# Attention: block maxima taken two at a time, row sums formed one unit later, heads divided in pairs

## The chip, the cores and the metric

The kernel runs on one core of one Trainium2 chip. The metric is the device time of one execution in microseconds (us); the median of the runs shown is 2695.03 us.

## The reference

One layer of a bidirectional encoder with 2048 tokens of width 1024, all in float32: a mixer sub-layer (8 query heads over 2 key heads of width 64, beside a pooling mixer, and one output projection) and a gated feed-forward sub-layer with a convolution of width 3. The change is in the attention:

```python
q = q * (1.0 / math.sqrt(HEAD_DIM))
s = jnp.einsum('bqkgd,bskd->bkgqs', qblk, k)
p = jax.nn.softmax(s, axis=-1)
o = jnp.einsum('bkgqs,bskd->bqkgd', p, v)
...
mix = jnp.concatenate([att, pool], axis=-1) @ w_out[l]
x = x + g1 * mix
h2 = rmsnorm(x, norm2_g[l]) * (1.0 + sc2) + sh2
```

The softmax needs three things for each query: the maximum of its 2048 scores, the exponentials' sum, and the weighted sum of the values divided by it.

## The kernel before, in words

Operands are split into a high part that TensorE takes exactly and a low rest, so that products come out close to float32. A stage ahead of the attention (spans 0 to about 380 us) projects queries, keys, values and pooled channels and writes them to DRAM; a stage behind it (from about 1240 us) is the feed-forward part.

The attention goes through 32 units: 4 chunks of 512 queries (QC) times 8 heads. `gen_unit(u)` walks over 16 blocks of 128 keys (kt). For each it makes the scores S in one of three banks of PSUM (L731, L732; the second matmul adds minus the row maximum, which sits in row 64 of `qb`), two exponentials on ScalarE (ph, rounded, L735, and the full one in place, L736), their difference pl on VectorE (L737), and two steps behind it the products with the values: `pv` adds ph times values into bank A (L723) and pl times values and ones into bank B (L724). The sum of ph over the keys goes two ways: GpSimd adds up the first 13 blocks in `acc` (L739, L741), and for the last three (ONE_PE) TensorE multiplies ph with ones into B (L726). At the unit's end acc is split into ah (ScalarE, L751) and al (VectorE, L752), and two more matmuls with ones add these to B (L757, L758). Then ScalarE copies half of A and the row of sums out of the banks (L765, L766), VectorE adds the halves into `o1` (L767, L768), and the row of sums goes through DRAM by four DMAs on SP's queue: out, back as 128x4, reciprocal on VectorE (L776), out, and back spread over 64 partitions as `rb` (L774 to L778). `finish(u)`, called in step 10 of the next unit, multiplies o1 by rb into one half of `att` (L798) and, with every second head, splits att into atth (ScalarE) and attl (GpSimd, L802).

`gen_max(u+1)` runs beside unit u, one step of it to each step of the unit: 16 matmuls pmx (4 query tiles times 4 blocks of 512 keys, L692), each into one of two banks with the tag mx, and each followed by a maximum over its 512 columns on VectorE (L694). Then the 16 partial maxima of the four query tiles become nm (L697), four small matmuls turn it into a row in a bank with the same tag (L701), and ScalarE copies that row into qb (L702). Without it the next unit's L732 cannot run.

Beside the units run the fillers of `plan`: matmuls of the output projection (`gen_half`, L820) into the one bank misc, whose result VectorE adds to x (L842), and `ln2_early`, the norm ahead of the feed-forward part: sum of squares on ScalarE (L849), root on GpSimd (L120, L121), scaling of a 128x1024 tile on VectorE (L853), and eight transposes on TensorE (tp, L860).

The Python generators give a written order. The framework's scheduler takes it as the priority and issues, on each engine, the first instruction that it takes to be ready at that time, so each engine's final order is fixed in the program and can differ from the written one. It also places every wait. A tile of a tag with `bufs=1` can be written again only when all that read the last one are done.

## Time and profile before

| | before |
|---|---|
| median of 3 runs | 2695.03 us (2693.51 to 2695.31) |
| the profiled execution | 2694.41 us |
| its span, first to last instruction | 2692.6 us |
| TensorE matmuls busy | 2577.8 us (96%) |
| VectorE, ScalarE, GpSimd busy | 1926.2, 1544.4, 1615.7 us |

The profiled execution lies 0.6 us below the median, and its span 1.8 us below its own time. The attention takes the stretch from 385 to 1240 us, 855 us for 32 units, which is 26.7 us for one; stretches are named by their start and end in this span. The durations of neighbouring matmuls overlap in the records: a matmul of 512 columns is shown with 0.40 us, but the next one starts 0.23 us behind it.

### The profile page before, as it was taken

Reading aid. Unit: us, or ns where it says so; the run is one execution under the profiler, and the core shown is the slowest. Engines: PE = TensorE matmul, PEld = TensorE weight load, DVE = VectorE, ACT = ScalarE, POOL = GpSimd, SP = SyncE. Lnnn points to the kernel's source line nnn. Section 1 sums busy time; section 2 is a strip of 40 time slices with the busy share of each in tenths; the row PEclk is TensorE's granted clock in tenths of the full one; section 3 lists DMA queues with packets and bytes.
Section 4 is the critical chain, followed back from the end, with each engine's and each line's share of the span. In section 5 each row is a group of like instructions: output and inputs, shape, how many; then the busy total and the mean of one; then the engine's idle time right before and its main releaser. Section 6 shows DMA issues by size and latency. Waiting matters only on the chain.

```text
span 2692.6 us, 38997 instructions
## 1 busy us (share of the span) xinstructions
PE 2577.8 (96%) x13439; PEld 2232.5 (83%) x13439; DVE 1926.2 (72%) x3014; ACT 1544.4 (57%) x2848; POOL 1615.7 (60%) x1397
## 2 busy tenths in 40 slices
PE   5899989999999999989899999899999999999999
PEld 5788877777776776767898999699999998999998
DVE  7877678889999999888577776745555557455554
ACT  5565457767778777776654555554343445544442
POOL 1222135656566666664887887586565676777673
PEclk9999989999999999999999999999999999999999
DMA  9685373431222122223544444533332325333332
GB/s 293 233 266 180 100 242 103 149 100 58 71 63 77 58 76 69 78 88 120 172 149 135 148 132 139 195 106 103 105 106 94 95 78 189 114 122 118 110 110 86
DMA packets 318161, 338.61 MB, mean 126 GB/s; under 512 B 24656, under 2 KB 226330, under 8 KB 317962
## 3 DMA queue, kind: packets, MB, share of 16 engines
q1 hardware_dynamic: 316953, 332.31, 39.1%
q0 software_dynamic: 1008, 3.81, 0.5%
q8 instruction: 105, 1.72, 0.3%
q14 instruction: 95, 0.77, 0.1%
HBM read 249.42 MB, written 86.63 MB: 125 GB/s over the span
## 4 chain that ended last, share of the span: by engine, by line
PE 47%; DVE 2%; POOL 1%; ACT 1%; issue 1%; DMA 0%; DVEq 0%; SPq 0%; POOLq 0%; ACTq 0%
PE py L1248 16%; PE px L1159 13%; PE pw L1159 9%; PE pz L1159 8%; PE pl L1377 1%; DVE b L993 0%; POOL wl_s L1035 0%; ACT hb L977 0%; POOL t L1000 0%; DVE y L1253 0%; DMA wr<-in_w_up_dram 0%; POOL t L1007 0%; POOL wl_a L1035 0%; ACT ac L1218 0%; DVE t L993 0%
## 5 line engine op out<-in xcount | busy, mean ns | idle before, releaser
L741 POOL TENSOR_TENSOR acc<-acc,ph 128x512 f32<-128x512 f32 x352 | 463.6, 1317 | 40.7 <-ACT ph L735 15.5
L1035 POOL TENSOR_TENSOR wl_s<-s,wh_s 128x512 fp32r<-128x512 f32 x260 | 349.6, 1346 | 204.7 <-ACT wh_s L1033 202.1
L735 ACT ACTIVATE ph<-S 128x512 fp32r<-128x512 f32 x512 | 306.9, 600 | 130.0 <-PE S L732 114.3
L737 DVE TENSOR_TENSOR pl<-S,ph 128x512 fp32r<-128x512 f32 x512 | 348.0, 683 | 40.0 <-ACT S L736 33.0
L1253 DVE TENSOR_TENSOR y<-py,y 128x512 f32<-128x512 f32 x300 | 205.8, 688 | 222.4 <-PE py L1248 220.7
L694 DVE TENSOR_REDUCE mx<-pmx 128x1 f32<-128x512 f32 x500 | 337.4, 680 | 25.9 <-PE pmx L692 23.9
L1033 ACT CAST wh_s<-s 128x512 fp32r<-128x512 f32 x264 | 163.5, 621 | 313.0 <-PE pw L1159 146.8
L1035 POOL TENSOR_TENSOR wl_a<-wr,wh_a 128x512 fp32r<-128x512 f32 x195 | 266.7, 1374 | 104.7 <-ACT wh_a L1033 104.3
L736 ACT ACTIVATE S<-S 128x512 f32<-128x512 f32 x512 | 306.5, 599 | 0.0
L1248 PE MATMUL py<-wdh,gh 128*128 128x512 f32 x664 | 261.7, 395 | 1.9 <-DVE y L1253 1.7
L1248 PE MATMUL py<-wdh,gl 128*128 128x512 f32 x664 | 262.1, 395 | 0.0
L1248 PE MATMUL py<-wdl,gh 128*128 128x512 f32 x664 | 261.8, 395 | 0.0
L1033 ACT CAST wh_a<-wr 128x512 fp32r<-128x512 f32 x198 | 122.3, 618 | 240.8 <-PE pz L1159 202.4
L1159 PE MATMUL px<-t,wh_s 128*128 128x322 f32 (+1 forms) x1024 | 247.9, 322 | 5.3 <-ACT p1s L1192 3.6
L724 PE MATMUL B<-pl,vt 128*128 128x512 f32 x512 | 210.5, 411 | 5.3 <-DVE pl L737 5.0
L723 PE MATMUL A<-ph,vt 128*128 128x512 f32 x512 | 204.6, 408 | 5.3 <-ACT ph L735 5.3
L692 PE MATMUL pmx<-kA,qa 128*128 128x512 f32 x500 | 203.2, 408 | 3.4 <-DMA kA<-k_scr 2.5
L732 PE MATMUL S<-qb,kB 65*128 65x512 f32 x512 | 202.8, 402 | 1.1 <-ACT qb L702 0.8
L731 PE MATMUL S<-qa,kA 128*128 128x512 f32 x512 | 202.4, 398 | 0.0
L739 POOL TENSOR_TENSOR acc<-ph,ph 128x512 f32<-128x512 f32 x32 | 41.3, 1290 | 255.4 <-ACT ph L735 234.9
L1159 PEld LDWEIGHTS px<-t,wh_s 128*128 128x128 f32 x1024 | 178.3, 189 | 12.3 <-ACT p1s L1192 4.4
L1159 PE MATMUL px<-t,wl_s 128*128 128x322 f32 (+1 forms) x512 | 164.2, 321 | 0.0
(297 smaller groups left out, 6877.9 us busy)
## 6 DMA issues: line engine op xcount, KB each, us to landing
wr<-in_w_up_dram SPq DMA_DIRECT2D x132, 512.0 KB
wdh<-wd_scr SPq DMA_DIRECT2D x88, 256.0 KB
wdl<-wd_scr SPq DMA_DIRECT2D x88, 256.0 KB
stage<-in_w_ada_dram SPq DMA_DIRECT2D x36, 512.0 KB
x_scr<-x SPq DMA_DIRECT2D x48, 256.0 KB
wds<-in_w_down_dram SPq DMA_DIRECT2D x44, 256.0 KB
wd_scr<-wdh SPq DMA_DIRECT2D x44, 256.0 KB
wd_scr<-wdl SPq DMA_DIRECT2D x44, 256.0 KB
```

Of the source, the lines that this page charges most:

```text
L694: V.tensor_reduce(out=mx[:, qt, j:j + 1], in_=ps, axis=AX.X, op=ALU.max)
L723: PE.matmul(A, vt[:, kt, 192 * a:192 * a + P], ph, start=kt == 0, stop=kt == NKT - 1)
L724: PE.matmul(B, vt[:, kt, 64 + 64 * a:192 + 64 * a], pl, start=kt == 0, stop=False)
L735: S.activation(out=ph, in_=s, func=AF.Exp, scale=0.125)
L736: S.activation(out=s, in_=s, func=AF.Exp, scale=0.125)
L737: V.tensor_tensor(out=pl, in0=s, in1=ph.bitcast(F32), op=ALU.subtract)
L741: G.tensor_tensor(out=acc, in0=acc, in1=ph.bitcast(F32), op=ALU.add)
L1033: S.copy(out=hf, in_=src)
L1035: eng.tensor_tensor(out=lf, in0=src, in1=hf.bitcast(F32), op=ALU.subtract)
L1159: mm = PE.matmul(ps, l_[:, k], r_[:, k, 0:N], start=first and k == 0 and m == 0, stop=k == 3 and m == 2, skip_group_check=not first)
L1248: PE.matmul(ps, l_[:, ts_], r_, start=i == 0, stop=i == 3 * len(js) - 1)
L1253: V.tensor_tensor(out=ys[t][:, ns], in0=ps, in1=ys[t][:, ns], op=ALU.add)
```

## The change

- `gen_max` takes pmx in pairs: two matmuls fill a tile of 2 x 512 columns (two banks, tag mx, now `bufs=1`), and one VectorE maximum goes over all 1024 columns. A unit has 8 such maxima instead of 16, and nm reads 8 columns instead of 16. The row of L701 takes a pair tile too.
- GpSimd adds up ph of all 16 blocks (ONE_PE applies to the last unit alone), and al is made on GpSimd instead of VectorE. The three matmuls per unit of ph with ones go.
- The two matmuls with ah and al no longer go into B at the unit's end. `sum_up(u-1)`, called in step 3 of the next unit, makes them into a pair tile of tag mx; ScalarE copies one row of it out, and DRAM now takes two rows (one from B, one from this tile), which come back as 128x2x4 and are added ahead of the reciprocal: five DMAs instead of four, and one more small VectorE instruction. ah and al keep their slots (tags ph with 4, pl with 3) until then.
- VectorE adds B straight into `att`; one multiplication 128x512 for two heads takes the place of two of 64x512, and `finish` comes in step 13 instead of 10.
- The scaling in `ln2_early` goes from VectorE to GpSimd.
- The last unit keeps the old way; two tail halves of the output projection wait for the last `sum_up`.

```diff
 
+        def mx_pair(nm):
+            return ps2.tile([P, 2, 512], F32, tag="mx", name=nm, bufs=1)
+
         def gen_max(u):
             c_, h = units[u]
             a = h // 4
             qa, qb = qtiles[u]
-            mx = p2.tile([P, 4, 4], F32, tag="mx", name=f"mx{u}", bufs=2) if u else mx0
-            for jq in range(0 if u else 4 * JP, 16):
-                for j, qt in ((jq // 4, jq % 4) if u == 0 else (jq % 4, jq // 4),):
-                    ps = ps2.tile([P, 512], F32, tag="mx", name=f"pmx{u}_{qt}_{j}", bufs=2)
-                    PE.matmul(ps, qa[:, qt * P:(qt + 1) * P], kA[:, a, j * 512:(j + 1) * 512],
+
+            def pair(nm):
+                return mx_pair(f"{nm}{u}")
+
+
+            mx = p2.tile([P, 4, 2], F32, tag="mx", name=f"mx{u}", bufs=2) if u else mx0
+            for i in range(8 if u else 2):
+                ps = pair(f"pmx{i}_")
+                for t in range(2):
+                    qt, j = (i // 2, 2 * (i % 2) + t) if u else (2 * i + t, JP)
+                    PE.matmul(ps[:, t], qa[:, qt * P:(qt + 1) * P], kA[:, a, j * 512:(j + 1) * 512],
                               start=True, stop=True)
-                    V.tensor_reduce(out=mx[:, qt, j:j + 1], in_=ps, axis=AX.X, op=ALU.max)
+                    if u == 0:
+                        V.tensor_reduce(out=mx[:, qt, j:j + 1], in_=ps[:, t], axis=AX.X, op=ALU.max)
                     yield
+                if u:
+                    V.tensor_reduce(out=mx[:, qt, i % 2:i % 2 + 1], in_=ps.rearrange("p a n -> p (a n)"),
+                                    axis=AX.X, op=ALU.max)
             nm = p2.tile([P, 4], F32R, tag="nm", name=f"nm{u}", bufs=2)
             V.tensor_reduce(out=nm, in_=mx, axis=AX.X, op=ALU.max, negate=True)
-            row = ps2.tile([P, 512], F32, tag="mx", name=f"row{u}", bufs=2)
+            row = pair("row")[:, 0]
             yield
             for qt in range(4):
                 PE.matmul(row[0:1, qt * P:(qt + 1) * P], nm[:, qt:qt + 1], identr, start=True, stop=True)
...
             first = []
+            final = u == NU - 1
 
             def pv(kt, ph, pl):
                 PE.matmul(A, vt[:, kt, 192 * a:192 * a + P], ph, start=kt == 0, stop=kt == NKT - 1)
-                PE.matmul(B, vt[:, kt, 64 + 64 * a:192 + 64 * a], pl, start=kt == 0, stop=False)
-                if kt >= NKT - ONE_PE:
+                PE.matmul(B, vt[:, kt, 64 + 64 * a:192 + 64 * a], pl, start=kt == 0,
+                          stop=kt == NKT - 1 and not final)
+                if final and kt >= NKT - ONE_PE:
                     PE.matmul(B, onesr[:, o64], ph, start=False, stop=False)
 
             for kt in range(NKT):
...
                 V.tensor_tensor(out=pl, in0=s, in1=ph.bitcast(F32), op=ALU.subtract)
                 if kt == 1:
                     G.tensor_tensor(out=acc, in0=first[0].bitcast(F32), in1=ph.bitcast(F32), op=ALU.add)
-                elif 1 < kt < NKT - ONE_PE:
+                elif 1 < kt < NKT - (ONE_PE if final else 0):
                     G.tensor_tensor(out=acc, in0=acc, in1=ph.bitcast(F32), op=ALU.add)
                 first.append(ph)
                 pend.append((kt, ph, pl))
...
             while pend:
                 if len(pend) == 1:
                     S.copy(out=ah, in_=acc)
-                    EA.tensor_tensor(out=al, in0=acc, in1=ah.bitcast(F32), op=ALU.subtract)
+                    (V if final else G).tensor_tensor(out=al, in0=acc, in1=ah.bitcast(F32), op=ALU.subtract)
                 pv(*pend.pop(0))
                 yield
-            for _ in range(XY):
-                yield
-            PE.matmul(B, onesr[:, o64], ah, start=False, stop=False)
-            PE.matmul(B, onesr[:, o64], al, start=False, stop=True)
+            if final:
+                PE.matmul(B, onesr[:, o64], ah, start=False, stop=False)
+                PE.matmul(B, onesr[:, o64], al, start=False, stop=True)
             dr = slice(64 * a, 64 * a + 64)
             rr = slice(64 - 64 * a, 128 - 64 * a)
             r0 = 64 - 64 * a
+            lo = 64 * (h % 2)
+            if h % 2 == 0:
+                att["f"] = p2.tile([P, QC], F32, tag="att", name=f"att{u}", bufs=1), \
+                    p2.tile([P, QC], F32, tag="rb", name=f"rb{u}", bufs=1)
+            at, rb = att["f"]
...
             S.copy(out=o1[dr], in_=A[rr])
             S.copy(out=o1[r0:r0 + 1], in_=B[r0:r0 + 1])
             V.tensor_tensor(out=o1[dr], in0=A[dr], in1=o1[dr], op=ALU.add)
-            V.tensor_tensor(out=o1[dr], in0=B[dr], in1=o1[dr], op=ALU.add)
...
+            V.tensor_tensor(out=at[lo:lo + 64], in0=B[dr], in1=o1[dr], op=ALU.add)
             SP.dma_start(out=r_scr[u, 0], in_=o1[r0:r0 + 1])
-            SP.dma_start(out=rc, in_=r_scr[u, 0].rearrange("o (p i) -> (o p) i", i=4))
-            V.reciprocal(out=rc, in_=rc)
-            SP.dma_start(out=r_scr[u, 1].rearrange("o (p i) -> (o p) i", i=4), in_=rc)
-            SP.dma_start(out=rb[dr], in_=r_scr[u, 1].broadcast_to([64, QC]))
-            open_units[u] = (o1, rb, dr)
-            yield
+            open_units[u] = (o1, dr, at, rb)
+            sums[u] = (ah, al, o64, r0)
+            yield
+
+        def sum_up(u):
+
+            ah, al, o64, r0 = sums.pop(u)
+            o1, dr, at, rb = open_units[u]
+            lo = 64 * (units[u][1] % 2)
+            rs = mx_pair(f"rs{u}")[:, 0]
+            PE.matmul(rs, onesr[:, o64], ah, start=True, stop=False)
+            PE.matmul(rs, onesr[:, o64], al, start=False, stop=True)
+            r1 = r0 + 32
+            S.copy(out=o1[r1:r1 + 1], in_=rs[r1:r1 + 1])
+            SP.dma_start(out=r_scr[u, 1], in_=o1[r1:r1 + 1])
+            rc = p2.tile([P, 2, 4], F32, tag="rc", name=f"rc{u}", bufs=2)
+            SP.dma_start(out=rc, in_=r_scr[u, 0:2].rearrange("n o (p i) -> (o p) n i", i=4))
+            V.tensor_tensor(out=rc[:, 0], in0=rc[:, 0], in1=rc[:, 1], op=ALU.add)
+            V.reciprocal(out=rc[:, 0], in_=rc[:, 0])
+            SP.dma_start(out=r_scr[u, 2].rearrange("o (p i) -> (o p) i", i=4), in_=rc[:, 0])
+            SP.dma_start(out=rb[lo:lo + 64], in_=r_scr[u, 2].broadcast_to([64, QC]))
+            if u == NU - 2:
+                last_sum.append(u)
 
...
-            E = V if u == NU - 1 else E1
-            E.tensor_tensor(out=at[lo:lo + 64], in0=o1[dr], in1=rb[dr], op=ALU.mult)
-            if h % 2 == 1:
-                S.copy(out=ah[:, h // 2], in_=at)
-                E = V if u == NU - 1 else E2
-                E.tensor_tensor(out=al[:, h // 2], in0=at, in1=ah[:, h // 2].bitcast(F32),
-                                op=ALU.subtract)
+            last = u == NU - 1
+            if last:
+                row = o1[64 - dr.start:65 - dr.start]
+                rl = ps2.tile([P, 512], F32, tag="A", name="rb_last", bufs=1)
+                PE.matmul(rl, ones[64 - dr.start:65 - dr.start, :], row, start=True, stop=True)
+                V.tensor_tensor(out=at[0:64], in0=at[0:64], in1=rb[0:64], op=ALU.mult)
+                V.tensor_tensor(out=at[64:128], in0=o1[dr], in1=rl[dr], op=ALU.mult)
+            else:
+                V.tensor_tensor(out=at, in0=at, in1=rb, op=ALU.mult)
+            S.copy(out=ah[:, h // 2], in_=at)
+            E = V if last else E2
+            E.tensor_tensor(out=al[:, h // 2], in0=at, in1=ah[:, h // 2].bitcast(F32), op=ALU.subtract)
...
-            V.tensor_scalar(out=x1, in0=x1, scalar1=r, scalar2=None, op0=ALU.mult)
+            eng.tensor_scalar(out=x1, in0=x1, scalar1=r, scalar2=None, op0=ALU.mult)
             for _ in range(wait[1]):
                 yield
             for q in range(2):
...
                     step(filler)
                     frac -= 1
-                if n == 10 and u > 0:
+                if n == 3 and u > 0:
+                    sum_up(u - 1)
+                if n == 13 and u > 0:
                     finish(u - 1)
                 if n == 2:
```

## Rows read from the trace of the kernel before

**Rows 1.** The page: busy time, share of the span and instructions of each engine.

```profile
PE 2577.8 (96%) x13439; PEld 2232.5 (83%) x13439; DVE 1926.2 (72%) x3014; ACT 1544.4 (57%) x2848; POOL 1615.7 (60%) x1397
```

**Rows 2.** Busy time by stretch: the attention's four quarters, and all of it.

```profile
core 0: us, PE busy (x) PEld busy (x) DVE busy (x) ACT busy (x) POOL busy (x), PEclk, DMA share, GB/s
385.00:600.00 215.00, 211.09 (x894) 163.89 (x894) 190.54 (x314) 155.50 (x287) 128.64 (x99) 0.98 0.44 140
600.00:816.00 216.00, 214.05 (x924) 165.62 (x922) 197.35 (x327) 162.05 (x302) 132.34 (x102) 1.00 0.23 69
816.00:1022.00 206.00, 198.32 (x845) 145.41 (x844) 191.62 (x316) 165.22 (x312) 135.62 (x112) 1.00 0.23 67
1022.00:1240.00 218.00, 208.18 (x888) 156.04 (x889) 189.58 (x307) 166.54 (x315) 135.76 (x114) 0.98 0.26 74
385.00:1240.00 855.00, 831.63 (x3548) 630.94 (x3548) 769.08 (x1260) 649.30 (x1216) 532.37 (x427) 0.99 0.29 88
```

**Rows 3.** Waits in 385 to 1240: us in total, times, longest.

```profile
PE tp L860 <- DVE lx L853: 6.0, 7, 2.0
PE A L723 <- ACT ph L735: 5.3, 16, 0.9
PE B L724 <- DVE pl L737: 5.0, 15, 0.6
PE po L820 <- DVE x L842: 0.4, 1, 0.4
...
DVE rc L776 <- DMA rc<-r_scr: 1.3, 2, 0.8
...
POOL acc L739 <- ACT ph L735: 234.9, 30, 10.8
```

**Rows 4.** Groups of 385 to 1240: count, busy us, mean ns, idle before, what ended it.

```profile
L741 POOL TENSOR_TENSOR acc<-acc,ph 128x512 f32<-128x512 f32 x352 | 463.6, 1317 | 40.7 <-ACT ph L735 15.5 <-PE pmx L692 0.9
...
L726 PE MATMUL B<-ph,onesr 128*128 128x512 f32 x96 | 38.0, 396 | 0.0
...
L798 DVE TENSOR_TENSOR att<-o,rb 64x512 f32<-64x512 f32 x31 | 36.8, 1186 | 0.7
...
L842 DVE TENSOR_TENSOR x<-po,x 128x512 f32<-128x512 f32 x48 | 32.6, 680 | 0.2
...
L752 DVE TENSOR_TENSOR al<-acc,ah 128x512 fp32r<-128x512 f32 x32 | 21.7, 679 | 0.0
L802 POOL TENSOR_TENSOR attl<-att,atth 128x512 fp32r<-128x512 f32 x15 | 19.3, 1288 | 0.0
...
L853 DVE TENSOR_SCALAR lx<-lx,rstd 128x1024 f32<-128x1024 f32 x12 | 11.0, 920 | 2.1 <-POOL rstd L121 2.1
```

**Rows 5.** Timeline of one unit's end: start, us, engine, line, operation, count, idle before.

```profile
628.38 0.40 PE L726 MATMUL B<-ph,onesr 128*128 128x512 f32 x1
628.61 0.40 PE L757 MATMUL B<-ah,onesr 128*128 128x512 f32 x1
628.85 0.40 PE L731 MATMUL S<-qa,kA 128*128 128x512 f32 x1
629.24 0.51 PE L758 MATMUL B<-al,onesr 128*128 128x512 f32 x1
629.58 0.40 PE L701 MATMUL row<-identr,nm 128*1 128x128 f32 x4
...
627.90 0.68 DVE L694 TENSOR_REDUCE mx<-pmx 128x1 f32<-128x512 f32 x1
628.50 0.68 DVE L752 TENSOR_TENSOR al<-acc,ah 128x512 fp32r<-128x512 f32 x1
629.10 0.16 DVE L697 TENSOR_REDUCE nm<-mx 128x4 fp32r<-128x16 f32 x1
...
629.78 0.58 ACT L766 COPY o<-B 1x512 f32<-1x512 f32 x1 [1.61 <-PE B L758]
630.38 0.57 ACT L702 CAST qb<-row 1x512 fp32r<-1x512 f32 x1
```

## What the change should do to the time

> **What bounds the kernel now.** I read the busy times first: TensorE's matmuls fill 96% of the span, no other engine more than 72% [rows 1]. Then the stretches of the attention [rows 2]: of 855 us TensorE is busy 831.6, the other 23 are lost in small pieces, and VectorE is next with 769, or 90%. VectorE's share overstates it: in the timeline its 512-column instructions are shown with 0.68 us and start 0.60 apart (627.90, 628.50, 629.10), so about a tenth of its rows is overlap [rows 5]. GpSimd is busy 62%. A matmul is shown with 0.40 us, and the next starts 0.23 behind it (628.38, 628.61, 628.85) [rows 5]; 0.23 is what one more or less costs while TensorE has work. Last come the waits: of the named ones of TensorE the largest are the transposes on the scaled tile, 6.0 us, ph, 5.3, and pl, 5.0 [rows 3]. So TensorE is the bound, and a matmul saved is time saved, except where TensorE waits anyway. That place is a unit's end [rows 5]: acc, split into ah and al, goes as matmul L758 into B, ScalarE's copy out of B (629.78) stands waiting for it 1.61 us, and the copy that gives the next unit its maxima (630.38) stands in ScalarE's queue behind that; TensorE's starts there are 0.39 and 0.34 apart instead of 0.23.
>
> **The matmuls.** Three per unit go (96 of L726 in 32 units [rows 4], 93 after the change took all but the last unit's). The ah and al matmuls stay, but move into the next unit. At 0.233: 93 x 0.233 = 21.7 us, if all of it is on the path. At the unit's end five matmuls go, 1.17 us, and two come back in the next unit's body, 0.47. What the end then waits for is VectorE: in [rows 5] the last maximum starts at 627.90, al at 628.50, nm at 629.10. Without al, nm can start 0.6 earlier, and the copy into qb no longer queues behind the copy out of B; that one took 0.58 from 629.78, so the row's copy comes about 0.9 earlier in all. If the end is bound by this chain, a unit gains 0.9 - 0.47 = 0.43 us, 13 us in 31 units; if TensorE's queue finds other work for the rest, 21.7. The written order need not be the issued one: in [rows 5] a score matmul of the next unit (628.85) already stands ahead of this unit's L758, so most holes are filled. I take 18.
>
> **The paired maxima.** The maximum over 1024 columns isn't in the trace. The same operation takes 0.68 on 512 and 0.16 on 16 columns [rows 5]; in a straight line that gives 0.68 + 512 x (0.68 - 0.16)/496 = 1.22 us, and start to start 1.14 instead of 2 x 0.60. That frees 8 x 0.06 = 0.5 us of VectorE per unit; al gives 0.60 more, and one multiplication of two heads instead of two (1.19 each [rows 4]) about 0.6; a small add of 128x4 costs under 0.16. Some 1.5 of 26.7 us. VectorE isn't the bound, so only waits for it shrink: those of L724 on pl, 5.0 us, and part of others [rows 3]. I take 3 us, between 0 and 10.
>
> **One pair tile instead of two banks.** This is the added wait. The first matmul of a pair must wait for the maximum over the pair ahead of it, and what is queued behind it on TensorE waits with it: the next scores, and so ScalarE and VectorE. From the start of a pair's second matmul the next pair can start after 0.40 (the matmul), some 0.3 (VectorE in the midst of a 0.60 instruction), 1.22 and a little: 1.96 us. In the written order there lie four matmuls of S, A and B and about 1.5 of filler between them, 5.5 x 0.233 = 1.28. The lack of 0.68 is covered if three more matmuls are issued in front. A unit has some 26 us for eight rounds of 0.23 + 1.96 = 2.2, 17.5 in all, the row and the new sums each one round more: there is room. The nearest row for one buffer handed back and forth is the misc bank: written 48 times behind VectorE's addition (L842 [rows 4]), TensorE waited 0.4 us for that in all [rows 3]. That rate on 248 pairs gives 2 us; I take 3, and keep 53 as the far end, which is 0.21 us for each of the 248, two matmuls moved in front and not three.
>
> The Trainium skill (PSUM — Partial Sum Buffer, Summary: rules for kernel authors) says to read PSUM in a different bank from the one that a running matmul targets. Both kernels keep to that, but before it was two buffers in turn and now it is two banks held as one buffer; by that rule alone this edit is a loss, and it is the first rival below.
>
> **GpSimd.** It gets three additions (1.317 each) and al (shape of attl, 1.288) per unit [rows 4]: 5.24 x 8 = 42 us per quarter, so 171 to 178 of 206 to 218 [rows 2]. The cover is its idle time ahead of each unit's first addition, 234.9 us in 30 waits, 7.8 each [rows 3]. If that cover were short, its lateness would hold ph's four slots (of which ah now keeps one for a third of a unit), and ScalarE behind them: 0 to 16 us. I take 0. Twelve scalings of 128x1024 move to it. Here they take 0.92 [rows 4]; GpSimd has none of that shape, two inputs of 512 take 1.3, so up to 2.6 for 1024, and no less than the 0.75 or so that the other engine takes undisturbed. So -2 to +20 us if every bit of it reaches the transposes, which waited for this tile 6.0 us [rows 3]; I take +3.
>
> The Trainium skill (GPSIMD Engine Reference, 4.1 Engine selection) gives elementwise work to VectorE, with GpSimd about 2 times slower on two inputs. The rows agree on al: 0.679 on VectorE, 1.288 on GpSimd. It calls one input roughly line rate, which for 1024 columns would be an estimate of 1.1 us, and my 3 would be 2.
>
> **What I cost at nothing.** The extra ScalarE copy per unit (0.58, 18 us in all) lies beside ScalarE's idle 24%. The fifth DMA and the later sums: the chain now starts some 9 us into the unit and has 10 us up to step 13 for two round trips; the reciprocal waited 1.3 us in 31 times [rows 3], and only every second unit needs the result in step 13. If the multiplication stood waiting on VectorE, pl and the maxima would queue behind it, some 2 us each time, 16 times, 32 us. SP's loads for units three ahead have room to be late. The last two tail halves and step 13 cost nothing for the same reason.
>
> **The sum.** -18 - 3 + 3 + 3 = -15 us. From the profiled execution, 2694.4, that is 2679.4; the median stands 0.6 higher, so 2680.0.
>
> **Rivals.** (1) The pair tile is the bound, slower: TensorE stands before each pair. For it: 0.68 us short in the written order, and the scheduler's order is fixed ahead, so what comes late by a tenth on the chip is waited for. Against it: the misc bank. It decides the sign from 18 us, 0.073 us a pair; at 0.21 it gives -18 - 3 + 53 + 3 = +35, 2730. (2) No change: GpSimd paces the units. Fifteen additions, al, half an attl and the wait for ah (0.6) make 19.8 + 1.3 + 0.6 + 0.6 = 22.3, in the last two quarters some 1.5 more, of 26.7; should each unit wait 0.5 us for it, 16 us go, and 2696 is left. That would also be the answer if the unit's end were limited by its chain and one other cost of the list came in full: 2680 + 5 + 11. (3) More than forecast: the chain from acc through B to the row's copy was what disturbed TensorE most, and with a lighter VectorE half of its lost 23 us comes back: -21.7 - 12 = -34, 2661. (4) Slower through the late scaling on GpSimd or the later sums, +20 or +32 less 15: 2690 to 2712.
>
> **Chances.** The forecast, about 8 to 25 us faster, 0.42; (3) 0.18; (2) 0.15; (1) 0.17; (4) 0.08, all but a little of it slower. A difference of under 0.2%, 5.4 us, can't be told from none. Faster 0.60, same 0.15, slower 0.25. The range takes in (2), (3) and (1) at its price and leaves out a worse loss or a bigger gain: 2656 to 2730. The forecast's own range is 2670 to 2687.
>
> **What would show it.** Right: 31 units shorter by 0.4 to 0.7 us; L726 left with three matmuls; a 1024-column maximum of about 1.22; waits of L692 on the maximum under 10 us; the copy into qb close behind its row; GpSimd's wait ahead of L739 down from 7.8 to some 2 to 3 us a unit. Wrong: waits of pmx on mx of tens of us, or ph waiting for acc for tens of us, the transposes for the scaled tile, or the multiplication of L798 for rb. The stages outside the attention must keep their lengths; if they don't, the forecast misses something that I haven't seen.

## The result: 3% slower, and the profile after

The changed kernel takes 2773.51 us (median of four runs, 2772.99 to 2780.99), the kernel before 2694.27 beside it: a ratio of 1.0301, 95% interval 1.0282 to 1.0319, or 79 us more. The forecast was 2680 with a range of 2656 to 2730: wrong in sign, and the time lies above the range.

| | before | after |
|---|---|---|
| span of the profiled execution | 2692.6 us | 2771.3 us |
| granted clock, mean | 0.988 | 0.975 |
| up to the attention's first score matmul | 378.3 us | 376.0 us |
| first to last score matmul of the attention | 856.8 us | 934.8 us |
| from there to the first feed-forward product | 39.4 us | 44.2 us |
| the rest | 1418.1 us | 1416.3 us |

Of the 78.7 us between the spans the 32 units have 78.0, or 2.4 us a unit. The last unit's end has 4.8 more, the other stages a little less than before. The page's first line, as in [rows 1], shows 93 matmuls fewer, as planned, VectorE relieved by 40 us, and GpSimd with 193 us more:

```profile
PE 2596.3 (94%) x13346; PEld 2226.5 (80%) x13346; DVE 1885.7 (68%) x2739; ACT 1563.2 (56%) x2879; POOL 1808.7 (65%) x1533
```

PE's busy time rose although its matmuls fell. That is mostly the clock: 326 matmuls start at its lower level in this kernel, 163 in the one before. The stretches of the attention's four chunks, as in [rows 2] (columns: stretch, its length, busy time and instructions of each engine, granted clock, DMA share, GB/s):

```profile
core 0: us, PE busy (x) PEld busy (x) DVE busy (x) ACT busy (x) POOL busy (x), PEclk, DMA share, GB/s
376.00:607.00 231.00, 214.84 (x879) 159.41 (x877) 184.74 (x250) 159.79 (x297) 167.04 (x132) 0.95 0.45 142
607.00:831.00 224.00, 212.73 (x889) 157.96 (x888) 185.92 (x253) 162.83 (x306) 175.59 (x136) 0.99 0.24 66
831.00:1069.00 238.00, 205.44 (x832) 145.62 (x830) 182.17 (x246) 172.57 (x325) 190.53 (x149) 0.95 0.21 60
1069.00:1316.00 247.00, 219.46 (x873) 160.09 (x874) 178.35 (x244) 173.40 (x325) 190.00 (x148) 0.92 0.20 60
376.00:1316.00 940.00, 852.46 (x3469) 623.09 (x3468) 731.18 (x990) 668.59 (x1248) 723.16 (x563) 0.95 0.27 82
```

GpSimd, the one that got more, is busy 723 of 940 us and so not full; TensorE is busy 852 of them, a smaller share than before. The loss grows to the end: the last two chunks are the slowest (238 and 247), and in them lie eleven of the twelve scalings. What TensorE, VectorE, ScalarE and GpSimd waited for between 385 and 1330 us (us in total, times, longest), against [rows 3]:

```profile
PE row L714 <- DVE nm L710: 27.6, 17, 4.4
PE tp L897 <- POOL lx L890: 16.9, 7, 4.8
PE S L748 <- ACT qb L715: 11.5, 13, 3.2
PE A L738 <- ACT ph L751: 6.0, 12, 1.7
PE po L857 <- DVE x L879: 5.8, 8, 1.4
PE pmx L701 <- DVE mx L707: 4.5, 9, 1.6
PE B L739 <- DVE pl L753: 3.3, 9, 0.6
DVE att L837 <- DMA rb<-r_scr: 1.4, 3, 0.9
ACT ah L767 <- POOL acc L757: 59.9, 31, 4.1
POOL acc L755 <- ACT ph L751: 114.1, 30, 13.5
POOL al L768 <- ACT ah L767: 17.5, 24, 0.7
```

The first line is new: the row of maxima waits for its VectorE result in 17 units (before: once, 1.0 us). So is the wait of ScalarE's copy ah for GpSimd's last addition, in all 31 units that add all 16 blocks on GpSimd (before: once, 0.3 us). The groups that answer to [rows 4] (count, busy us, mean ns, idle before and what ended it):

```profile
L707 DVE TENSOR_REDUCE mx<-pmx 128x1 f32<-128x1024 f32 x248 | 301.7, 1216 | 79.0 <-PE pmx L701 78.6
L890 POOL TENSOR_SCALAR lx<-lx,rstd 128x1024 f32<-128x1024 f32 x12 | 34.3, 2859 | 1.2
L768 POOL TENSOR_TENSOR al<-acc,ah 128x512 fp32r<-128x512 f32 x31 | 39.7, 1282 | 17.5 <-ACT ah L767 17.5
L701 PEld LDWEIGHTS pmx<-kA,qa 128*128 128x128 f32 x497 | 92.2, 197 | 46.6 <-DVE mx L707 15.7 <-ACT o L807 11.7 <-DVE mx L704 1.3
```

The fourth line is easily missed. In the list of waits a matmul pmx waits 4.5 us for maxima, but its weight load, which comes first on the engine, waits 15.7 for maxima and 11.7 for the copy of the late sums (L807), which sit in the same tile: a wait can stand at the load and not at the matmul. Now one unit's end in the timeline, as in [rows 5] (start, us, engine, operation, idle before):

```profile
898.90 1.29 POOL L757 TENSOR_TENSOR acc<-acc,ph 128x512 f32<-128x512 f32 x1
...
900.22 0.62 ACT L767 CAST ah<-acc 128x512 fp32r<-128x512 f32 x1 [2.14 <-POOL acc L757]
900.86 0.59 ACT L783 COPY o<-A 64x512 f32<-64x512 f32 x1
901.48 0.68 DVE L785 TENSOR_TENSOR o<-A,o 64x512 f32<-64x512 f32 x1 [1.96 <-ACT o L783]
902.09 1.21 DVE L707 TENSOR_REDUCE mx<-pmx 128x1 f32<-128x1024 f32 x1
903.33 0.68 DVE L792 TENSOR_TENSOR att<-B,o 64x512 f32<-64x512 f32 x1
904.04 0.16 DVE L710 TENSOR_REDUCE nm<-mx 128x4 fp32r<-128x8 f32 x1
904.35 0.40 PE L714 MATMUL row<-identr,nm 128*1 128x128 f32 x4 [2.57 <-DVE nm L710]
904.79 0.58 ACT L715 CAST qb<-row 1x512 fp32r<-1x512 f32 x1 [2.74 <-PE row L714]
```

Read it from the top: GpSimd ends its last addition at 900.19. ScalarE's ah stands next in ScalarE's order and has waited 2.14 us for it; the copy of A stands behind ah; VectorE's addition behind that copy; the last maximum behind that addition, though its matmuls were done long before (the pair at 899.53); then nm, the row, which TensorE waits 2.57 us for, and qb, without which no score of the next unit ends. An addition on GpSimd, which no product of this unit needs any more, has become the head of the chain into the next unit through the fixed orders of two other engines. Over the 31 units the addition ends 2.70 us behind the end of the sixteenth ph (before: 2.17 ahead of it), nm starts 4.10 behind it (before 2.56), and the next unit's first score matmul on qb 6.49 (before 4.79).

**A budget of TensorE's time.** Since waits stand in several places, I added them up at one: in the attention (from 20 us behind the first score matmul to 3 us behind the last), each start-to-start distance of neighbouring matmuls beyond 0.2335 us (0.11 for the narrow ones), booked to the matmul that starts late; what is due to a granted clock of 0.5 is booked apart. Records that are missing count as lost, so a few us are uncertain.

| us lost | all | half clock | row | pmx | tp | S | A, B | po |
|---|---|---|---|---|---|---|---|---|
| before | 48.9 | 2.0 | -3.9 | 3.7 | 10.5 | 7.8 | 22.5 | 4.8 |
| after | 143.6 | 16.9 | 25.7 | 23.0 | 20.8 | 17.8 | 25.5 | 12.6 |

After has lost 94.7 us more. Less 93 matmuls at 0.2335, 21.7, that makes 73.0 of the 78.0, so in this account the saved matmuls were paid out in full and the losses are over four times as large. They are the row (+30), pmx (+19), half clock (+15), tp (+10), S (+10) and po (+8). Three parts of the change can be behind them: three more blocks on GpSimd, the one pair tile, and the scaling on GpSimd. The experiments take them one by one.

### The profile page after: what moved, and what is told of

The parts are those of the page before. It is cut to its first block, busy times and chain, and to the rows that moved or that the text cites. A ratio compares the mean times of both kernels' runs of the same rounds, so it can differ in the third digit from the quotient of the medians.

```text
span 2771.3 us, 38990 instructions
## 1 busy us (share of the span) xinstructions
PE 2596.3 (94%) x13346; PEld 2226.5 (80%) x13346; DVE 1885.7 (68%) x2739; ACT 1563.2 (56%) x2879; POOL 1808.7 (65%) x1533
## 4 chain that ended last, share of the span: by engine, by line
PE 45%; DVE 2%; POOL 1%; ACT 1%; issue 1%; DMA 0%; DVEq 0%; POOLq 0%; ACTq 0%
PE py L1295 15%; PE px L1206 12%; PE pw L1206 8%; PE pz L1206 8%; PE pl L1424 1%; DVE b L1040 0%; POOL wl_s L1082 0%; ACT hb L1024 0%; POOL t L1047 0%; DVE y L1300 0%; POOL wl_a L1082 0%; POOL t L1054 0%; DVE ac L1268 0%; DMA h_scr<-ht 0%; DMA wr<-in_w_up_dram 0%
## 5 line engine op out<-in xcount | busy, mean ns | idle before, releaser
L757 POOL TENSOR_TENSOR acc<-acc,ph 128x512 f32<-128x512 f32 x445 | 578.4, 1300 | 69.4 <-ACT ph L751 40.9
L707 DVE TENSOR_REDUCE mx<-pmx 128x1 f32<-128x1024 f32 x248 | 301.7, 1216 | 79.0 <-PE pmx L701 78.6
L748 PE MATMUL S<-qb,kB 65*128 65x512 f32 x512 | 212.2, 415 | 12.3 <-ACT qb L715 11.5
L738 PE MATMUL A<-ph,vt 128*128 128x512 f32 x512 | 214.8, 426 | 7.5 <-ACT ph L751 6.0
L701 PE MATMUL pmx<-kA,qa 128*128 128x512 f32 x500 | 182.9, 426 | 11.6 <-DVE mx L707 4.5
L120 POOL TENSOR_SCALAR rstd<-ss 128x1 f32<-128x1 f32 (+1 forms) x48 | 20.0, 416 | 207.7 <-ACT junk L276 100.9
```

The lines of the kernel that those rows point to most:

```text
L707: V.tensor_reduce(out=mx[:, qt, i % 2:i % 2 + 1], in_=ps.rearrange("p a n -> p (a n)"), axis=AX.X, op=ALU.max)
L738: PE.matmul(A, vt[:, kt, 192 * a:192 * a + P], ph, start=kt == 0, stop=kt == NKT - 1)
L748: PE.matmul(s, kB[0:65, a, ks], qb[0:65], start=False, stop=True)
L757: G.tensor_tensor(out=acc, in0=acc, in1=ph.bitcast(F32), op=ALU.add)
```

## Experiments: one part taken back from the changed kernel

Each kernel is given with its ratio to the kernel before, timed beside it. The diffs of this section stand against the changed kernel.

**The three blocks back on TensorE in every unit** (the late sums and al stay as changed):

```diff
-                if final and kt >= NKT - ONE_PE:
-                    PE.matmul(B, onesr[:, o64], ph, start=False, stop=False)
+                if kt >= NKT - ONE_PE:
+                    PE.matmul(B, onesr[:, o64], ph, start=False, stop=kt == NKT - 1 and not final)
...
-                elif 1 < kt < NKT - (ONE_PE if final else 0):
+                elif 1 < kt < NKT - ONE_PE:
```

> The kernel after with ONE_PE = 3 in every unit: GpSimd adds up 13 blocks again and TensorE multiplies the last three ph with ones into B, 93 matmuls more than after. Theory 1 (GpSimd is late: its last addition ends 2.7 us behind the unit's last ph, ScalarE's copy ah stands waiting for it 59.9 us in 31 units, and the copies of A, VectorE's additions, the last maximum and the row stand behind it): the wait of ah on acc goes to a few us, the stretch from a unit's last ph to the next unit's first comes back from 7.7 to about 6 us, and the time falls by 40 to 55 us less up to 20 for the matmuls: 2715 to 2745. Theory 2 (the pair tile with one buffer is what makes the row late): no gain, 2775 to 2795. Theory 3 (the scaling on GpSimd): GpSimd has 4 us less per unit, a little gain, 2760 to 2775.

Measured: 2752.18 us, 1.0219 (1.0199 to 1.0239), 21 us faster with 93 matmuls more. The wait of ah for the addition falls from 59.9 us to 0.5, that of the row from 27.6 to 8.2:

```profile
ACT ah L767 <- POOL acc L757: 0.5, 2, 0.3
PE row L714 <- DVE nm L710: 8.2, 8, 1.6
```

So the additions cost the 21 us and beside them the 21.7 that the matmuls had saved by the budget's price: some 43 us.

**The maxima again over 512 columns in two banks:**

```diff
-            return ps2.tile([P, 2, 512], F32, tag="mx", name=nm, bufs=1)
+            return ps2.tile([P, 512], F32, tag="mx", name=nm, bufs=2)
...
-                if u:
-                    V.tensor_reduce(out=mx[:, qt, i % 2:i % 2 + 1], in_=ps.rearrange("p a n -> p (a n)"),
-                                    axis=AX.X, op=ALU.max)
+                    V.tensor_reduce(out=mx[:, qt, j:j + 1], in_=ps, axis=AX.X, op=ALU.max)
```

> The kernel after with maxima of 512 columns one at a time in two banks again; the sums' tile and the row take one bank of that tag. All else as after. Theory 1: the row still stands behind ah, 2760 to 2785, with VectorE's extra 0.5 us per unit hidden. Theory 2: the loss is the pair tile's, 2700 to 2725. Theory 3: 2765 to 2780.

Measured: 2759.87 us, 1.0244 (1.0228 to 1.0260), 14 us faster. VectorE is busier, and the kernel is faster: the pair tile costs more than its shorter maxima bring. The row waits less (27.6 us in the changed kernel), and the transposes wait more (16.9 there), so a part of the gain is lost again:

```profile
PE row L705 <- DVE nm L701: 17.5, 15, 2.3
PE tp L888 <- POOL lx L881: 26.1, 8, 6.5
```

**The scaling back on VectorE:**

```diff
-                               lambda nm: ps2.tile([P, 512], F32, tag="misc", name=nm, bufs=1), p2, LW, G)
+                               lambda nm: ps2.tile([P, 512], F32, tag="misc", name=nm, bufs=1), p2, LW, V)
```

> The kernel after with the scaling of the twelve 128x1024 tiles on VectorE again (GpSimd took 2.86 us for each, TensorE's transposes waited 16.9 us for it). Theory 1 and theory 2: only that wait and a part of GpSimd's lateness in the last two quarters, 2745 to 2765. Theory 3: most of the loss, 2700 to 2730, and the first two quarters, which have no scaling, unchanged either way.

Measured: 2747.08 us, 1.0199 (1.0183 to 1.0215), 26 us faster for twelve instructions. TensorE's wait for the scaled tile falls from 16.9 to 6.9 us:

```profile
PE tp L897 <- DVE lx L890: 6.9, 7, 1.8
```

**ah and al written behind the next unit's maxima** (acc is kept until then), so that ScalarE need not stand before GpSimd's last addition:

```diff
+        def split_acc(u):
+            ah, al = sums[u][0:2]
+            acc = accs.pop(u)
+            tc.keep_in_program_order(S.copy(out=ah, in_=acc))
+            G.tensor_tensor(out=al, in0=acc, in1=ah.bitcast(F32), op=ALU.subtract)
```

> The kernel after with the split of acc (ah on ScalarE, al on GpSimd) written behind the row's copy into qb and kept there in ScalarE's order, so that nothing of the unit's end is queued behind a wait for GpSimd. GpSimd does all that it does in the kernel after. Theory 1: the stretch from the last ph to the next unit's first falls from 7.7 to 6 us or less, 2773 - 50 = 2720, between 2705 and 2740. Theory 2: the row is late because of the pair tile, not of ah: 2765 to 2780. Theory 3: the same, 2765 to 2780.

Measured: 2759.03 us, 1.0244 (1.0224 to 1.0264), 14.5 us faster. The wait falls from 59.9 to 7.0 us:

```profile
ACT ah L802 <- POOL acc L757: 7.0, 5, 2.2
```

But the issued order was only half of what was written: in 30 of 31 units ah stands behind the copies of A and B and still ahead of qb's copy, so the row waits 15.6 us instead of 27.6, and not the 8.2 of the run above. A written order is not an issued one; the trace has to be read for it.

No single part explains the 79 us: taken back alone they give 21, 14 and 26, 61 together. So I put the takebacks together.

## Experiments: parts taken back together, and the account closed

**All three back** (the edits of the first three runs): what is left of the change is the late sums, al on GpSimd and the division in pairs. No edit of its own.

> The kernel after with GpSimd's sum back to 13 blocks (as in e1), the scaling on VectorE (e3) and maxima of 512 columns (e2). What stays: al on GpSimd, row sums in a bank of the maxima in the next unit, five DMAs, heads in pairs. Additive theory: 2773.5 - 21.3 - 26.4 - 13.6 = 2712, between 2703 and 2720. Theory that these three are the whole loss: 2685 to 2697, as before. Theory that the later row sums cost most: 2725 or more.

Measured: 2699.07 us, 1.0023 (1.0013 to 1.0032), 5 us behind the kernel before. The row's wait is nearly gone, and the first score of a unit waits little for qb:

```profile
PE row L705 <- DVE nm L701: 2.2, 5, 0.7
PE S L739 <- ACT qb L706: 7.0, 8, 3.1
```

**The same, but with the pair tile kept:**

> e6 with the paired maxima of the kernel after kept: GpSimd's sum of 13 blocks, scaling on VectorE, pair tile, which here also takes the row sums. Against e6 (2699) it gives the pair's price beside the new sums. If the pair costs what it cost alone on the kernel before (25 us): 2718 to 2728; if VectorE's relief by al and the joined multiplication pays for a part: 2703 to 2715; if the new sums in the same tile make it worse: over 2730.

Measured: 2728.87 us, 1.0131 (1.0112 to 1.0149). With that the way from before to after is a chain of kernels in which each step after the first adds one part:

| | us | step | lost in the budget |
|---|---|---|---|
| before | 2694.3 | | 48.9 |
| + late sums, al on GpSimd, heads in pairs | 2699.1 | +5 | 54.3 |
| + pair tile | 2728.9 | +30 | 75.6 |
| + three blocks on GpSimd, 93 matmuls fewer (the run with the scaling on VectorE) | 2747.1 | +18 | 116.2 |
| + scaling on GpSimd: the changed kernel | 2773.5 | +26 | 143.6 |

The steps make the 79 us by construction; what they show is that no step of the chain is a gain, and that the third hides a loss of about 40 behind 21.7 us of matmuls (116.2 - 75.6). The order in which the parts are added matters: the pair tile is worth 14 us when taken back from the changed kernel and 30 in the chain.

**The better chain, the scaling and the maxima together** (the edits of the second, third and fourth run; the 93 matmuls stay saved):

> The kernel after with three parts undone or moved at once: ah and al behind the row's copy (as in e4), the scaling on VectorE (as in e3), maxima of 512 columns in two banks (as in e2). What stays of the change: 93 matmuls fewer, 15 additions and al on GpSimd, the row sums in the next unit, heads in pairs. Additive theory (each of the three costs what its own undoing gave: 14.5, 26.4 and 13.6 us): 2773.5 - 54.5 = 2719, between 2710 and 2728. Theory that they hide one another (GpSimd's lateness shows at whichever place is left): all three gone, the matmuls saved show, 2675 to 2700. Theory that the rest of the change costs most: 2735 or more.

Measured: 2712.51 us, 1.0076 (1.0048 to 1.0104). Without pair tile and with the scaling on VectorE the additions on GpSimd still turn 21.7 us of saved matmuls into a loss of 18 (5 of it the late sums and what goes with them). What is late now is the next step of the chain, qb, with ah still ahead of it on ScalarE:

```profile
PE S L739 <- ACT qb L706: 18.7, 16, 3.0
```

## Experiments: one part alone in the kernel before

**The pair tile alone.** The maxima as changed, everything else as before (two tail halves wait for the last row, as they must with one tile):

```diff
-                    ps = ps2.tile([P, 512], F32, tag="mx", name=f"pmx{u}_{qt}_{j}", bufs=2)
+                ps = mx_pair(f"pmx{i}_{u}")
...
-            row = ps2.tile([P, 512], F32, tag="mx", name=f"row{u}", bufs=2)
+            row = mx_pair(f"row{u}")[:, 0]
```

> The kernel before with the paired maxima alone (one tile of two banks, 1024 columns in one maximum; the two tail halves that use this tile wait for the last row). Theory that the pair tile by itself makes the row later at a unit's end (a maximum over two blocks can start only behind the second, and then takes 1.22 us and not 0.68): nm later by about 0.5 to 0.8 us, 31 units, 2693 + 15 to 25 = 2708 to 2718. Theory that it costs only behind the late sums of the kernel after: 2688 to 2698.

Measured: 2718.29 us, 1.0093 (1.0068 to 1.0119): 25 us, with no part of GpSimd touched (the profiled execution is the longest of the four, 2722.9). From the list of waits one would not guess it: the wait named there for the matmuls pmx is 5.0 us. The budget finds 18.5 us lost ahead of pmx against 3.7, and 7.8 more in half clock. The weight loads show the direction (before, then this kernel; the same stretch, 380 to 1312):

```profile
L692 PEld LDWEIGHTS pmx<-kA,qa 128*128 128x128 f32 x500 | 95.7, 192 | 30.9 <-DVE mx L694 8.3 <-DMA kA<-k_scr 3.2
```
```profile
L696 PEld LDWEIGHTS pmx<-kA,qa 128*128 128x128 f32 x500 | 92.7, 195 | 45.3 <-DVE mx L702 18.0 <-DVE mx L699 3.9 <-DMA kA<-k_scr 3.6
```

25 us for 248 hand-overs is 0.10 us each in the mean; they are not alike, some 7 us of the loss stand ahead of the sixth pair of a unit and under 1 ahead of the last. The one buffer and the maximum twice as long come together in every run, so no run prices them apart. The Trainium skill (PSUM — Partial Sum Buffer, Summary: rules for kernel authors) says to read PSUM in a different bank from the one that a running matmul targets. Both kernels keep to that, so the rule by itself does not make this edit a loss, as the prediction took it to. What the 25 us of this run price is something else, two banks held as one buffer in place of two buffers in turn.

**Is it the last maximum, twice as long just where the row waits for it?** The last pair is reduced as two halves of 512, and the partial maxima become nm in two small instructions; the rest of that kernel is unchanged:

```diff
+                    elif i == 7:
+                        V.tensor_reduce(out=mx[:, 3, 1 + t:2 + t], in_=ps[:, t], axis=AX.X, op=ALU.max)
...
-                if u:
+                if u and i < 7:
```

> e7 (the kernel before with paired maxima) with one edit: the last pair of a unit is taken as two maxima of 512 columns, the first as soon as the first matmul is done; the partial maxima become nm in two small instructions. The seven other pairs keep the one buffer. Theory that e7's 25 us come from the last maximum, which starts behind the second matmul and lasts 1.22 us: nm returns from 3.2 to about 2.7 us behind the last ph, 2718 - 10 to 18 = 2700 to 2708. Theory that they come from handing the one buffer back and forth in the unit's body: 2713 to 2720.

Measured: 2724.79 us, 1.0113 (1.0100 to 1.0126): no gain. The time lost ahead of pmx stays (17.9 us) and with it the time. But the split did not do what it was for: the last nm starts 3.4 us behind the unit's last ph, 3.2 before the split, so the run alone does not clear the last maximum. What speaks for the hand-over of the tile in the unit's body is the budget of the kernel with the pair tile alone: 14.8 us more ahead of pmx, nearly all of them ahead of pairs other than the last, but under 2 more ahead of the row and under 3 ahead of S.

**The scaling alone:**

```diff
-            V.tensor_scalar(out=x1, in0=x1, scalar1=r, scalar2=None, op0=ALU.mult)
+            eng.tensor_scalar(out=x1, in0=x1, scalar1=r, scalar2=None, op0=ALU.mult)
```

> The kernel before with the scaling of the twelve 128x1024 tiles on GpSimd alone. GpSimd takes 2.86 us for each instead of VectorE's 0.92, 12 x 1.94 = 23 us longer in front of the transposes. Theory that this wait stands on TensorE's path in any kernel: 2693 + 15 to 25 = 2708 to 2718. Theory that it costs where GpSimd is already late with the sums: 2693 to 2703.

Measured: 2733.48 us, 1.0155 (1.0136 to 1.0174): 40 us for twelve instructions, more than the 26 they cost in the changed kernel. They take 2.86 us each, 34 us in all. For nine of the twelve tiles at most two matmuls start between the start of the scaling and the first transpose, so TensorE stands waiting for most of it:

```profile
PE tp L860 <- POOL lx L853: 31.1, 9, 4.7
```

The budget books 24 us more to tp, 12 to half clock and 6 to po: 41 in all. The stretch 800 to 1060 shows it for all engines at once, before first, then this kernel:

```profile
800.00:1060.00 260.00, 250.16 (x1068) 182.04 (x1068) 241.51 (x398) 210.11 (x397) 169.38 (x140) 1.00 0.24 70
```
```profile
800.00:1060.00 260.00, 232.69 (x952) 173.33 (x951) 211.36 (x345) 187.25 (x353) 167.69 (x131) 0.94 0.23 68
```

In equal time TensorE does 952 matmuls instead of 1068 and the other engines do less too; when TensorE stands before a transpose, scores, exponentials and maxima stand behind it.

**Can the wait be covered by writing the transposes ten steps behind the scaling instead of four?**

```diff
-        LW = (4, 4)
+        LW = (4, 10)
```

> e8 (the kernel before with the scaling on GpSimd) with LW = (4, 10) in place of (4, 4): the eight transposes are written six filler steps later. GpSimd still takes 2.86 us for each tile. Theory that e8's 40 us are TensorE standing before transposes that the schedule put too close behind the scaling (36 us of such waits in e8, 6 before): those waits fall under 12 us and the time to 2700 to 2712. Theory that GpSimd's 34 us more are what costs, by its own queue: 2725 to 2735.

Measured: 2729.40 us, 1.0130 (1.0116 to 1.0144). The wait, which should have fallen under 12 us, is 27.1: the issued order did not follow the written one. The first transpose of six tiles stands at the same place among the score matmuls as in the kernel above, that of the other six 1 to 8 score matmuls earlier, none later.

```profile
PE tp L860 <- POOL lx L853: 27.1, 9, 4.1
```

Whether an order with the transposes really later would cover the scaling was not tried.

## Experiments: is there a version with fewer matmuls that gains?

In the kernel with all three parts back (2699.1) TensorE sums three blocks of each unit. I gave one of them to GpSimd, and then two:

```diff
-        ONE_PE = 3
+        ONE_PE = 2
```

> e6 with ONE_PE = 2 in place of 3: GpSimd adds 14 blocks, TensorE multiplies the last two ph with ones, 31 matmuls fewer than e6. In e6 GpSimd's last addition ends 2.3 us ahead of the unit's last ph; one more takes 1.4, so ah still need not wait. Theory that a saved matmul is saved time while GpSimd is in time: 2699 - 7 = 2692. Theory that GpSimd's additions cost in any case (they hold ph's slots): 2699 to 2705.

Measured: 2702.94 us, 1.0030 (1.0019 to 1.0042). GpSimd's last addition still ends ahead of the last ph, by 0.6 us in the mean, and ah waits for it in four units only:

```profile
ACT ah L758 <- POOL acc L748: 5.5, 4, 1.9
```

```diff
-        ONE_PE = 3
+        ONE_PE = 1
```

> e6 with ONE_PE = 1: GpSimd adds 15 blocks, 62 matmuls fewer than e6. GpSimd's last addition ends about 0.5 us behind the last ph, where ah starts in e6. Theory that a saved matmul is saved time while GpSimd is in time: -14 and a few us of waits of ah back, 2686 to 2692. Theory that lateness counts from here: wait of ah on acc of 5 to 20 us in all, 2697 to 2706.

Measured: 2708.28 us, 1.0046 (1.0031 to 1.0061). 31 and 62 matmuls fewer are worth 7 and 14 us, and the kernels are 4 and 9 us slower than with none fewer. So the price sets in with the first block and is no threshold at the third: about 11 us for the first, 24 for two. (A loss of 4 us lies within the two kernels' intervals, a gain of 7 does not.) For the first block the price can't be the wait of ah, which is 5.5 us in all.

**ah really behind qb.** The issue of ah is tied to qb's copy of the next unit, first in the changed kernel:

```diff
+            qbs[u] = S.copy(out=qb[64:65, :], in_=row[0:1, :])
...
+            with tc.issue_after(qbs[u + 1].ins):
+                S.copy(out=ah, in_=acc)
```

> e4 done as it was meant. In e4 the split was written behind the row's copy but issued ahead of it: ScalarE's order in 28 of 31 units was copies of A and B, ah, row's copy, so the row still stood behind the wait for GpSimd. Here ah is tied behind the row's copy into qb; everything else as after. Theory that the wait for GpSimd in ScalarE's queue is what GpSimd's three additions cost: the time falls to e1's, 2752 less up to 20 for the matmuls saved, 2735 to 2750. Theory that GpSimd's lateness comes back by another way (ph's and pl's slots, al and with it the new sums later): 2755 to 2765, as e4.

Measured: 2762.21 us, 1.0260 (1.0242 to 1.0277). The row's wait falls as wanted, and two others rise: GpSimd stands waiting for ah before it can make al, and TensorE's transposes wait longer for the scaled tiles.

```profile
PE row L714 <- DVE nm L710: 10.3, 9, 1.7
PE tp L905 <- POOL lx L898: 29.2, 9, 5.3
POOL al L804 <- ACT ah L803: 87.2, 28, 4.5
```

Of the 17 us won at the row the transposes took 12 (16.9 before this edit, 29.2 behind it), and the kernel is 11 us faster than the changed one, not 20, and no faster than with the half order (2759.0). Most of the 12 us is the issued order again: for three tiles the transposes stand 3 or 4 score matmuls earlier in it than in the changed kernel, and those three wait 8 us longer.

**The same without pair tile and with the scaling on VectorE** (the run of 2712.5 with the order now as intended):

> e5 done as it was meant: ah behind the row's copy, scaling on VectorE, maxima of 512 columns; 93 matmuls fewer than e6 and three more additions on GpSimd. If the queue is all that the additions cost: e6's 2699 - 18 = 2681, between 2678 and 2690, which would be faster than before. If GpSimd's lateness comes back by another way: 2700 to 2715.

Measured: 2700.98 us, 1.0031 (1.0021 to 1.0040), 11.5 us better than the half order. The order of ah and qb on ScalarE was therefore a cause, and not all of it; with it right, 93 matmuls fewer should have given 2677 (2681 at the 18 us that I took for them) and didn't. The budget has 76.1 us lost, 27.2 more than before, against 21.7 saved: 9.6 more in S, 7.6 in half clock, 4.6 in pmx, 4.6 in the row. GpSimd's al waits for ah, 68.7 us in 30 units, but TensorE stands behind al for under 1 us, so that is no cost by itself:

```profile
POOL al L795 <- ACT ah L794: 68.7, 30, 5.4
```

**One block left on TensorE, ah behind qb:** the edit just shown, in the kernel with ONE_PE = 1.

> e11 (15 blocks on GpSimd, the last on TensorE, scaling on VectorE, maxima of 512 columns) with ah behind the row's copy. 62 matmuls fewer than e6. If the queue is all that the additions cost: 2699 - 14 = 2685, between 2682 and 2692. If not: 2700 to 2710.

Measured: 2697.18 us, 1.0010 (1.0000 to 1.0020), 11 us better than without the tie, and no different from before within what can be told. This is the best of all versions with fewer matmuls. No version that I ran beats the kernel before.

What stays open is where the rest went: some 24 us of the run before this one (2699.1 less 93 matmuls would be 2677.4) and some 12 of this one (less 62, 2684.6). Against the kernel with all three parts back, which has the late sums too, the budget of the former has 21.8 us more, and no one place holds them: half clock, the transposes and A have 4 to 5 each, S, the row and pmx about 2 each. ah and al hold one of four slots of ph and one of three of pl for longer than before, which could make the next unit's first exponentials and scores late; but most of the rise of S against before is already in the kernel with all three parts back. More slots were not tried. One rival the traces answer: GpSimd's longer hours do not stretch VectorE's instructions. pl takes 683 ns in the kernel before and 684 in the changed one, each the mean of 512.

## Why the prediction was wrong, step by step

**TensorE is the bound, a matmul saved is time saved: borne out by the account, by no run.** In the budget the 93 matmuls count with the 21.7 us of the upper bound (I took 18). This is bookkeeping that closes to 5 us, not an experiment: no run takes them away without putting work on GpSimd. Two readings of the kernel before were off. The 23 us that I called lost are the time without a matmul record; the records overlap, and the budget finds 48.9. And the unit's end that I read is not the common one: in 18 of 31 units the copy into qb is issued ahead of the copy out of B, so that the wait for L758 does not stand in front of it.

**Paired maxima: right in size.** The 1024-column maximum takes 1216 ns, worked out was 1.22. TensorE's wait for VectorE that I named, that of B on pl, fell from 5.0 to 3.3 us, within the 0 to 10 that I allowed.

**One pair tile: the first step that failed.** I took 3 us of a bracket of 0 to 53; it is 25 alone and 30 in the chain. The lever was the choice of the nearest row: the misc bank, whose named matmul wait was 0.4 us in 48 hand-overs [rows 3]. The wait that the list names at a matmul is not what a hand-over costs. Here the named wait of pmx is 5 us where the start-to-start distances hold 18.5, because much of it stands at the weight load (18.0 us there). The row was not a bad one, only read by the wrong measure: in the budget of before, po has lost 4.8 us, or 0.10 for each of the 48 hand-overs, 2.1 of them ahead of the first matmul behind a hand-over; on 248 pairs that would have been 11 to 25 us. The arithmetic beside it (1.96 us needed, 1.28 written in between, 0.68 short) was the better guide: with two matmuls moved in front it left 53 us, and half of that came.

**GpSimd at nothing: the second step that failed, and the largest.** The cover I named, 7.8 us of idle time in each unit [rows 3], is real and did shrink (114.1 us in 30 waits, 3.8 each). But it lies at the unit's start, ahead of the first addition; the additions that I put there run at the unit's end, the last of them from 1.4 us behind the last ph, and nothing idle in front of them can be used, since they need ph. Their lateness, 2.7 us, reaches the critical chain through ScalarE's fixed order, by ah. I had costed lateness as held slots, 0 to 16 us; the three blocks cost some 40. The way by ah is shown for a part of that: tying ah behind qb gave 11 us in each of the three kernels where I did it, some 24 of the price of the three blocks are left then, and the first block costs about 11 with hardly a wait of ah. The cause of that rest is open. The rival on GpSimd had the wait for ah in its sum, with 0.5 us a unit; 40 us in 31 units are 1.3.

**The scaling at +3, bracket -2 to +20: outside the bracket.** The instruction takes 2.86 us, over the bound of 2.6 from two inputs of 512, which a trace of before couldn't show. Above that I let it cost at most its own excess (12 times 1.7); it costs 26 to 40. The budget of the scaling alone shows what I left out beside the wait of the transposes: 12 us of half clock and 6 ahead of po. The Trainium skill (GPSIMD Engine Reference, 4.1 Engine selection) has one input at roughly line rate, an estimate of 1.1 us here; the trace shows 2.86 and decides.

**At nothing: late sums, the fifth DMA, step 13, al on GpSimd.** Nearly right: 5 us for all of it (2699.1 to 2694.3, the kernel with three parts back). VectorE waits 1.4 us for rb. What I missed lies behind the last unit: the way to the feed-forward part is 2.6 us longer in that kernel and 4.8 in the changed one. The division of the last two heads together is not it, since att, atth and attl start 1.1, 1.9 and 2.5 us behind the matmul rb_last in all three kernels, and the time goes behind them; on what, was not tested.

**The rivals.** The pair tile (0.17), GpSimd (0.15) and the scaling (0.08) were each priced as if it came alone, against a sum with all else as forecast. All three came at once, and a range that ends at the dearest single one, 2730, can't hold their sum. With the bounds as I had them, all bad ends together were 2694.4 - 18 - 3 + 53 + 16 + 20 = 2762. What the three have in common should have made me add them: each puts a producer later in a fixed order and TensorE, at 96% busy, stands behind all of them.

**What would show it.** Of the signs named as wrong, the transposes on the scaled tile came (16.9 us), ph waiting for acc only at the edge (10.2 us, 7.1 before), the multiplication hardly waiting for rb (1.4); of those named as right, L726 (L742 now) with three matmuls, the length of the maximum and the copy qb 0.44 us behind its row, and these said nothing on the time. GpSimd's wait ahead of the first addition fell to 3.8 us a unit, not to 2 to 3, and the units are longer by 2.4 us where they should have been shorter by 0.4 to 0.7. The waits of pmx under 10 us looked right and misled: 4.5 named, 23 lost.

## What to carry to other kernels

Idle time of an engine is cover only where it lies behind the inputs and ahead of the need; work moved to an idle engine at the end of a loop body can lengthen the hand-over to the next, and an in-order engine that has to copy its result passes the lateness on to everything behind that copy. Cost a buffer that is handed back and forth, or an instruction moved ahead of the bound engine, by the start-to-start times of the bound engine and not by its named waits, and add up the risks that make the same engine wait. In this kernel, where VectorE is not the bound, two buffers of one bank were worth more than one longer instruction over both.

## What the runs showed of the hardware that I had not expected

- GpSimd's multiplication of 128x1024 by one value per partition takes 2.86 us (2859 ns mean of 12), VectorE's 0.92 [rows 4]; GpSimd's addition of two 128x512 inputs takes 1.3. One input is not cheaper per column there than two.
- TensorE's granted clock fell to 0.5, the lower of its two levels, behind many waits of a few us, not behind all. Between 370 and 1320 us the kernel before runs at that level for 34 us, 20 of them at the start; the changed kernel for 89 us in ten stretches, and each of the nine behind the first begins in a hole ahead of a row, a transpose or a score, or about 1 us behind it; the holes are 1.9 to 4.8 us from matmul to matmul. Other holes of 2.6 and 3.0 us, the one in the timeline above among them, are followed by no fall. One of the nine, at the row of 1225 us (stretches before, in and behind the hole):

```profile
1212.00:1220.75 8.75, 8.21 (x36) 5.59 (x34) 7.81 (x11) 7.39 (x15) 8.28 (x8) 1.00 0.28 73
1220.75:1225.50 4.75, 0.40 (x2) 0.00 (x0) 1.66 (x4) 2.20 (x4) 3.74 (x4) 0.86 0.48 170
1225.50:1234.40 8.90, 7.85 (x23) 5.72 (x24) 4.11 (x6) 5.02 (x11) 6.14 (x5) 0.50 0.11 30
1234.40:1243.00 8.60, 8.60 (x39) 6.45 (x38) 6.98 (x10) 8.40 (x17) 7.61 (x6) 1.00 0.26 82
```

  23 matmuls in 8.9 us at 0.50, 39 in 8.6 at 1.00: the hole of 4.8 us costs some 3 more behind it (23 matmuls would take 5.4 at full clock, and part of the rest is a wait for qb). The budget books 17 us to that in the changed kernel and 2 before. That the hole is the cause is read from the order of events; no run changed the clock by itself.
